# Grouping wide and narrow matmuls by block in the feed-forward products of a two-layer decoder trunk, and building its tables at a later block

## The chip, the cores and the metric

The kernel runs on one core of one Trainium2 chip. The metric is the device time of one execution in microseconds (us). The core has five engines that run their own instruction streams and wait for one another through semaphores: TensorE (PE in the profile; its weight loads are listed as PEld), VectorE (DVE), ScalarE (ACT), GpSimd (POOL) and SyncE (SP), which here only issues DMAs. About 0.2% is what a measurement of this kernel can tell from no change.

## The reference

Two layers work on 256 tokens of width 1024. Each layer is a feed-forward part, a token mixer and a second feed-forward part, each added to the running x. The mixer of layer 0 is a dilated sliding-window attention, that of layer 1 a multi-head latent attention.

```python
D_MODEL, SEQ, DEPTH, D_FF = 1024, 256, 2, 2816

def swiglu(x, w_in, w_out):
    gate, up = jnp.split(x @ w_in, 2, axis=-1)
    return (jax.nn.silu(gate) * up) @ w_out

for i in range(DEPTH):
    x = x + 0.5 * swiglu(rmsnorm(x, norm_gains[i, 0]), ffn_w_in[i, 0], ffn_w_out[i, 0])
    h = rmsnorm(x, norm_gains[i, 1])
    y = dilated_window_attention(h, ...) if i == 0 else latent_attention(h, ...)
    x = x + y
    x = x + 0.5 * swiglu(rmsnorm(x, norm_gains[i, 2]), ffn_w_in[i, 1], ffn_w_out[i, 1])
```

The attention layers also need rotary tables (sines and cosines of the token positions times learned gains).

## The kernel before

**Precision.** Products are taken in a rounded 32-bit format. To keep accuracy, each operand is split into a rounded part `hi` and the rest `lo`: ACT casts a loaded weight piece to `hi` (line 107), DVE subtracts it from the raw piece to get `lo` (line 108). The activations are split in the same way and lie side by side, 256 columns of the rounded part and 256 of the rest. A product then needs two matmuls for each 128x128 weight tile: a **wide** one, in which the `hi` weights meet all 512 columns, and a **narrow** one, in which the `lo` weights meet only the 256 columns of the rounded part. Both add into the same bank of PSUM.

**Stages.** `trunk_kernel` runs a feed-forward part, the dilated attention, two feed-forward parts in a row, the latent attention, and a last feed-forward part. So there are four feed-forward stages, and `ffn` is called four times (lines 1035, 1037, 1039, 1041).

**One feed-forward stage.** The 2816 hidden columns are 22 blocks of 128. For each block `up(c)` takes one weight piece of 1 MB and makes 16 wide and 16 narrow matmuls: 8 slices k of the 1024 inputs, and for each the gate and the up weights (u = 0, 1). `taken` (lines 238, 240) and `gate` (lines 244 to 251) then turn the PSUM sums into the hidden activations `hh`. `down(sweep, q)` takes four hidden blocks and multiplies them into four of the eight output slices: again 16 wide (line 266) and 16 narrow (line 274) matmuls for one weight piece of 1 MB. The first sweep of `down` is interleaved with the `up` blocks, one after every fourth; its last piece and the second sweep follow the last block. I call one `up(c)`, or one full `down`, a **unit**: 16 wide and 16 narrow matmuls.

**Order on PE.** In three of the stages the matmuls of a unit alternate: wide, narrow, wide, narrow. The last stage sets `grouped=True`, and its `up` goes wide, wide, narrow, narrow. `down` alternates in all stages.

**Norm of the input.** The factor of the RMS norm is applied to the product, after the fact, so `up` can start before it is known. Inside early blocks `midway` puts `stats` (line 176: a sum over partitions on PE, then line 178 on DVE and a power on POOL, line 180) and `spread_rstd` (line 187 on DVE, line 189 on PE, line 191 on DVE). In the first stage both are in the third block, at k = 0 and k = 4; in the others they are in the second and third block at k = 4.

**Tables.** `setup` (lines 353 to 418) loads constants, gains and positions, and builds the rotary tables in about fifty small DVE instructions and two ACT ones. It is called by the hook of the first stage ahead of block 4.

**What sets the order.** The Tile framework allocates buffers (4 raw pieces, 3 `hi`, 3 `lo`, 2 PSUM tiles of two banks for `up`) and orders each engine's instructions by its own schedule, except for those that the first stage pins with `keep_in_program_order`. So an instruction can stand earlier or later on its engine than in the program. Each engine then runs its own list strictly in that order.

Of the kernel before, what the change touches and what calls it, by code (L numbers as in the profile page):

```python
# [30 lines left out]
P = 128  # L31
S = 256
D = 1024
KT = D // P
DFF = 2816
NC_FF = DFF // P
# [16 lines left out]
class Trunk:  # L53
# [82 lines left out]
    def squares(self, d0, xs, in_order=False, pinned=False):  # L136

        nc = self.nc
        n = xs.shape[1]
        sq = self.st.tile([P, 2, S], F32, name="sq")  # L140
        if in_order:
            nc.scalar.activation(
                sq[:, :n, :].rearrange("p d (a b) -> p d b a", b=4), xs.rearrange("p d (b a) -> p d b a", b=4), AF.Square
            )
        else:
            self.pin(pinned, nc.scalar.activation(sq[:, :n, :], xs, AF.Square))
        if d0 == 0:
            self.ssq = self.st.tile([P, S], F32, name="ssq")
            nc.gpsimd.tensor_tensor(self.ssq, sq[:, 0, :], sq[:, 1, :], op=ALU.add)
        else:  # L150
            for i in range(n):
                nc.gpsimd.tensor_tensor(self.ssq, self.ssq, sq[:, i, :], op=ALU.add)
# [38 lines left out]
        nc.vector.tensor_copy(self.bc, ps[:, :S])  # L191


    def ffn(self, up_w, out_w, done, first=None, hook=None, grouped=False):
        nc, tc = self.nc, self.tc
        with (
            tc.tile_pool(name="ff", bufs=2) as ff,
            tc.tile_pool(name="hh", bufs=NC_FF) as hp,
            ExitStack() as banks,
        ):  # L200

            acc_banks = self.banks(banks, "acc", 4)
            up_banks = self.banks(banks, "up", 2, other=True)
            self.small = lambda: acc_banks.tile([P, 512], F32, name="acc")
            hs = {}
            xs, xh = self.xs, self.xh

            pieces = {}

            def fetch(c, ahead=None, pinned=False):  # L210
                pieces[c] = self.piece(up_w[c], 4 if c < 6 else 1, ahead, pinned)

            def up(c, midway=()):
                if c not in pieces:
                    fetch(c)
                hi, lo = pieces.pop(c)
                hv, lv = (t.rearrange("p (k u c) -> p k u c", k=KT, u=2) for t in (hi, lo))

                ps = up_banks.tile([P, 2, 2, S], F32, name="up")
                for k in range(KT):  # L220
                    both = xs[:, k].rearrange("p t s -> p (t s)")
                    for part, u in ((0, 0), (0, 1), (1, 0), (1, 1)) if grouped else ((0, 0), (1, 0), (0, 1), (1, 1)):
                        if part == 0:
                            nc.tensor.matmul(  # L224
                                ps[:, u].rearrange("p t s -> p (t s)"), hv[:, k, u, :], both, start=k == 0, stop=False, skip_group_check=True
                            )
                        else:
                            nc.tensor.matmul(  # L228
                                ps[:, u, 0, :], lv[:, k, u, :], xh[:, k, :], start=False, stop=k == KT - 1, skip_group_check=True
                            )  # L230
                    for at, what in midway:
                        if k == at:
                            what()
                return ps

            def taken(ps, pinned=False):
                rest = ff.tile([P, 2, S], F32, name="rest")
                self.pin(pinned, nc.scalar.copy(rest, ps[:, :, 1, :]))  # L238
                gu = ff.tile([P, 2, S], F32, name="gu", bufs=4)
                self.pin(pinned, nc.vector.tensor_tensor(gu, ps[:, :, 0, :], rest, op=ALU.add))  # L240
                return gu

            def gate(c, gu):
                nc.vector.tensor_tensor(gu, gu, self.bc.unsqueeze(1).broadcast_to([P, 2, S]), op=ALU.mult)
                sg = ff.tile([P, S], F32, name="sg")
                nc.scalar.activation(sg, gu[:, 0, :], AF.Silu)
                h = ff.tile([P, S], F32, name="h")
                nc.vector.tensor_tensor(h, sg, gu[:, 1, :], op=ALU.mult)  # L248
                hs[c] = hh = hp.tile([P, 2, S], F32R, name="hh")
                nc.scalar.copy(hh[:, 0, :], h)  # L250
                nc.vector.tensor_tensor(hh[:, 1, :], h, hh.bitcast(F32)[:, 0, :], op=ALU.subtract)  # L251

            def down(sweep, q, accs, finish=None):

                cs = range(4 * q, min(4 * q + 4, NC_FF))
                hi, lo = (
                    t[:, : len(cs) * 512].rearrange("p (c d) -> p c d", d=512)  # L260
                    for t in self.piece(out_w[sweep][:, 4 * q * 512 : (cs[-1] + 1) * 512])
                )

                def term(c, d):
                    ds = slice(d * P, (d + 1) * P)
                    nc.tensor.matmul(  # L266
                        accs[d].rearrange("p t s -> p (t s)"),
                        hi[:, c - cs[0], ds],
                        hs[c].rearrange("p t s -> p (t s)"),
                        start=c == 0,  # L270
                        stop=False,
                        skip_group_check=True,
                    )
                    nc.tensor.matmul(  # L274
                        accs[d][:, 0, :], lo[:, c - cs[0], ds], hs[c][:, 0, :], start=False, stop=c == NC_FF - 1, skip_group_check=True
                    )

                if not finish:
                    for c in cs:
                        for d in range(4):  # L280
                            term(c, d)
                    return
                for ds in finish:
                    for d in ds:
                        for c in cs:
                            term(c, d)
                    done(sweep * 4 + ds[0], len(ds), [accs[d] for d in ds], 0.5)

            gus = {}
            if first:  # L290

                begin, squares = first
                fetch(0, begin, True)
                sums = up(0)
                squares(0)
                squares(1)
                fetch(1, None, True)
                squares(2)
                squares(3)
                gus[0] = taken(sums, True)  # L300
                sums = up(1)
                fetch(2, None, True)
                gus[1] = taken(sums, True)
                sums = up(2, ((0, lambda: self.stats(True)), (4, lambda: self.spread_rstd(True))))
                fetch(3, None, True)
                gus[2] = taken(sums, True)
            else:
                for c, what in enumerate((None, self.stats, self.spread_rstd)):
                    gus[c] = taken(up(c, ((KT // 2, what),) if what else ()))
            for c in range(3):  # L310
                gate(c, gus.pop(c))
            accs = None
            for c in range(3, NC_FF):
                if hook and c == 4:
                    hook()
                gate(c, taken(up(c)))
                if c % 4 == 1:
                    accs = accs or [acc_banks.tile([P, 512], F32, name="acc").rearrange("p (t s) -> p t s", t=2) for _ in range(4)]
                    down(0, c // 4 - 1, accs)
            down(0, 5, accs, ((0, 1), (2, 3)))  # L320
            pairs = [up_banks.tile([P, 2, 2, S], F32, name="up") for _ in range(2)]
            accs = [pairs[d // 2][:, d % 2] for d in range(4)]
            for q in range(5):
                down(1, q, accs)
            down(1, 5, accs, ((0,), (1,), (2,), (3,)))
# [673 lines left out]
def trunk_kernel(ctx: ExitStack, tc: tile.TileContext, x, pos, cst, ident, gtab, up, down, a_qk, a_v, a_out, b_in, b_kv, b_q, b_out, out):  # L999
    nc = tc.nc  # L1000
    t = Trunk(ctx, tc)
# [19 lines left out]
    def then_norm(gcol, order_from=False, order_to=False, columns=S):  # L1021
        def finish(d0, n, acc, scale):
            t.g = gcol
            t.place(columns)
            xs = t.residual(d0, n, acc, scale, order_from)
            t.split_x(d0, xs, order_to)
            t.squares(d0, xs, order_to)

        return finish
# [8 lines left out]
    t.side = "right"  # L1038
    t.ffn(up[2], down[2], then_norm(32, order_to=True))
    t.latent(b_in, b_kv, b_q, b_out, then_norm(40, order_from=True))  # L1040
    t.ffn(up[3], down[3], store, grouped=True)

# [84 lines left out]
```

## Time and profile before

| | us |
|---|---|
| median of 3 runs | 1159.91 (1158.91 to 1160.2) |
| the profiled execution: time | 1159.64 |
| the profiled execution: span, first to last instruction | 1157.9 |
| PE busy | 1141.0 (99% of the span) |
| DVE busy | 847.2 (73%) |
| ACT busy | 644.4 (56%) |

The profile gives, for each instruction, its start and length. Matmuls are pipelined: the start-to-start distance of two of them is what one costs, while the recorded length also holds its way through the array. "idle before" is the time in which the engine stood still ahead of an instruction, and behind the arrow is the instruction whose end let it go on. The granted clock is the share of TensorE's full clock; its mean over the run is 0.997.

### The profile page before, as it was taken

The page shows a single profiled execution, that of the slowest core. Times are in us where ns is not written, and L with a number is a line of the kernel's source. Part 1 is how long each engine was busy: PE and PEld are TensorE (multiplying, and loading weights), DVE is VectorE, ACT ScalarE, POOL GpSimd, SP SyncE. Part 2 cuts the span into 40 slices and gives each one's busy share as a digit, 9 for nine tenths or more (in the row PEclk, how much of TensorE's full clock was granted, in tenths as well). Part 3 has the DMA queues.
Part 4 walks back from the last instruction along what each step waited for, and adds up shares of the span by engine and source line. Part 5 has one row for each costly group of instructions (what it writes and reads, how often), then busy time and mean ns, then how long its engine had stood idle before and what let it go on. Part 6 is the DMA issues. An engine that isn't in the chain of part 4 may idle for free. (4 is left out here: it accounts for less than half of the span.)

```text
span 1157.9 us, 17729 instructions
## 1 busy us (share of the span) xinstructions
PE 1141.0 (99%) x6940; PEld 981.4 (85%) x6940; DVE 847.2 (73%) x1517; ACT 644.4 (56%) x1097; POOL 108.8 (9%) x99
## 2 busy tenths in 40 slices
PE   9899999999999999999999999999999899999998
PEld 8788888787888888888888888888888788888887
DVE  7866666888787977776666686666776897766673
ACT  6554545657566565654554464554555876555541
POOL 2000001221111211200000110000013212000000
PEclk9999999999999999999999999999999999999999
DMA  8555455554444344265555556554443334555550
GB/s 322 215 182 187 166 191 184 186 178 177 151 145 140 121 160 164 80 213 182 185 184 173 190 178 202 193 188 164 164 154 111 110 112 181 182 188 197 177 177 24
DMA packets 29747, 196.20 MB, mean 169 GB/s; under 512 B 3424, under 2 KB 4192, under 8 KB 7136
## 3 DMA queue, kind: packets, MB, share of 16 engines
q1 hardware_dynamic: 29376, 194.55, 48.5%
q8 instruction: 54, 0.88, 0.3%
q10 hardware_dynamic: 288, 0.52, 0.2%
q14 instruction: 29, 0.24, 0.1%
HBM read 194.01 MB, written 1.05 MB: 168 GB/s over the span
## 5 line engine op out<-in xcount | busy, mean ns | idle before, releaser
L108 DVE TENSOR_TENSOR lo<-raw,hi 128x512 fp32r<-128x512 f32 (+3 forms) x412 | 448.6, 1117 | 225.5 <-ACT hi L107 224.5
L107 ACT CAST hi<-raw 128x512 fp32r<-128x512 f32 (+3 forms) x412 | 376.7, 955 | 233.5 <-PE up L224 62.5
L224 PE MATMUL up<-xs,hi 128*128 128x512 f32 x1408 | 489.0, 400 | 1.8 <-DVE xs L134 1.3
L228 PE MATMUL up<-xs,lo 128*128 128x256 f32 x1408 | 367.0, 281 | 2.9 <-DVE lo L108 2.8
L224 PEld LDWEIGHTS up<-xs,hi 128*128 128x128 f32 x1408 | 253.5, 189 | 52.1 <-DVE xs L134 2.4
L228 PEld LDWEIGHTS up<-xs,lo 128*128 128x128 f32 x1408 | 267.2, 190 | 20.5 <-DVE lo L108 4.5
L266 PE MATMUL acc<-hh,hi 128*128 128x512 f32 x352 | 124.9, 395 | 0.0
L266 PE MATMUL up<-hh,hi 128*128 128x512 f32 x352 | 124.3, 394 | 0.3 <-DVE xg L163 0.3
L547 PE MATMUL acc<-hi,xs 128*128 128x512 f32 (+1 forms) x320 | 121.1, 379 | 0.0
L549 PE MATMUL acc<-hi,xs 128*128 128x512 f32 (+1 forms) x320 | 118.5, 370 | 0.0
L548 PE MATMUL acc<-lo,xs 128*128 128x512 f32 (+1 forms) x320 | 118.3, 370 | 0.0
L250 ACT CAST hh<-h 128x256 fp32r<-128x256 f32 x88 | 35.6, 406 | 140.5 <-DVE h L248 140.5
L274 PE MATMUL up<-hh,lo 128*128 128x256 f32 x352 | 99.5, 283 | 0.0
L274 PE MATMUL acc<-hh,lo 128*128 128x256 f32 x352 | 98.9, 282 | 0.0
L266 PEld LDWEIGHTS acc<-hh,hi 128*128 128x128 f32 x352 | 66.0, 188 | 16.0 <-DVE hh L251 1.0
L266 PEld LDWEIGHTS up<-hh,hi 128*128 128x128 f32 x352 | 66.1, 188 | 15.8 <-DVE xg L163 0.9
L547 PEld LDWEIGHTS acc<-hi,xs 128*128 128x128 f32 x320 | 60.3, 188 | 10.9 <-ACT vc L539 0.9
L549 PEld LDWEIGHTS acc<-hi,xs 128*128 128x128 f32 x320 | 60.3, 188 | 9.8
L548 PEld LDWEIGHTS acc<-lo,xs 128*128 128x128 f32 x320 | 60.3, 189 | 9.2
L274 PEld LDWEIGHTS up<-hh,lo 128*128 128x128 f32 x352 | 66.2, 188 | 0.2
L274 PEld LDWEIGHTS acc<-hh,lo 128*128 128x128 f32 x352 | 65.9, 188 | 0.0
L240 DVE TENSOR_TENSOR gu<-up,rest 128x512 f32<-128x512 f32 x88 | 60.1, 683 | 1.5 <-ACT rest L238 1.4
(195 smaller groups left out, 1339.1 us busy)
## 6 DMA issues: line engine op xcount, KB each, us to landing
raw<-in_up SPq DMA_DIRECT2D x87, 1024.0 KB, 4.9
raw<-in_down SPq DMA_DIRECT2D x40, 1024.0 KB, 4.8
raw<-in_a_qk SPq DMA_DIRECT2D x24, 1024.0 KB, 4.9
raw<-in_a_v SPq DMA_DIRECT2D x12, 1024.0 KB, 4.8
raw<-in_down SPq DMA_DIRECT2D x8, 512.0 KB, 3.5
raw<-in_a_out SPq DMA_DIRECT2D x4, 1024.0 KB, 4.8
raw<-in_b_out SPq DMA_DIRECT2D x4, 1024.0 KB, 4.8
raw<-in_b_in SPq DMA_DIRECT2D x3, 1024.0 KB, 5.1
```

The source lines that it names most:

```text
L107: self.pin(pinned, nc.scalar.copy(hi[:, c], raw[:, c]))
L108: self.pin(pinned, nc.vector.tensor_tensor(lo[:, c], raw[:, c], hi.bitcast(F32)[:, c], op=ALU.subtract))
L224: nc.tensor.matmul(ps[:, u].rearrange("p t s -> p (t s)"), hv[:, k, u, :], both, start=k == 0, stop=False, skip_group_check=True)
L228: nc.tensor.matmul(ps[:, u, 0, :], lv[:, k, u, :], xh[:, k, :], start=False, stop=k == KT - 1, skip_group_check=True)
L240: self.pin(pinned, nc.vector.tensor_tensor(gu, ps[:, :, 0, :], rest, op=ALU.add))
L250: nc.scalar.copy(hh[:, 0, :], h)
L266: nc.tensor.matmul(accs[d].rearrange("p t s -> p (t s)"), hi[:, c - cs[0], ds], hs[c].rearrange("p t s -> p (t s)"), start=c == 0, stop=False,
L274: nc.tensor.matmul(accs[d][:, 0, :], lo[:, c - cs[0], ds], hs[c][:, 0, :], start=False, stop=c == NC_FF - 1, skip_group_check=True)
L547: nc.tensor.matmul(out, xh, hi[:, k, :], start=kk == 0, stop=False)
L548: nc.tensor.matmul(out, xh, lo[:, k, :], start=False, stop=False)
L549: nc.tensor.matmul(out, xl, hi[:, k, :], start=False, stop=kk == KT - 1)
```

## The change

Four things are edited.

1. `up` of every block but the first makes all 16 wide matmuls and then all 16 narrow ones. The first block of a stage goes slice by slice in k, each with two wide and then two narrow ones.
2. `down` makes all wide matmuls of a piece first and then all narrow ones; in the last, half-size pieces it does so for each group of output slices that is finished together.
3. The callbacks of `midway` now run behind the narrow matmuls of their slice k, which stand in the second half of a block.
4. The hook of the first stage, which builds the tables, is called ahead of block 12 instead of block 4. The `grouped` flag goes.

```diff
-                for k in range(KT):
-                    both = xs[:, k].rearrange("p t s -> p (t s)")
-                    for part, u in ((0, 0), (0, 1), (1, 0), (1, 1)) if grouped else ((0, 0), (1, 0), (0, 1), (1, 1)):
...
-                    for at, what in midway:
-                        if k == at:
-                            what()
+                def term(k, u, part):
...
+                for ks in [(k,) for k in range(KT)] if c == 0 else [range(KT)]:
+                    for part in range(2):
+                        for k in ks:
+                            for u in range(2):
+                                term(k, u, part)
+                            if part == 1:
+                                for at, what in midway:
+                                    if k == at:
+                                        what()
...
+                def terms(pairs):
+                    for c, d in pairs:
+                        nc.tensor.matmul(
+                            accs[d].rearrange("p t s -> p (t s)"),
+                            hi[:, c - cs[0], d * P : (d + 1) * P],
...
+                    for c, d in pairs:
+                        nc.tensor.matmul(
+                            accs[d][:, 0, :],
+                            lo[:, c - cs[0], d * P : (d + 1) * P],
...
                 if not finish:
-                    for c in cs:
-                        for d in range(4):
-                            term(c, d)
+                    terms([(c, d) for c in cs for d in range(4)])
                     return
                 for ds in finish:
-                    for d in ds:
-                        for c in cs:
-                            term(c, d)
+                    terms([(c, d) for d in ds for c in cs])
                     done(sweep * 4 + ds[0], len(ds), [accs[d] for d in ds], 0.5)
...
-                if hook and c == 4:
+                if hook and c == 12:
                     hook()
...
-    t.ffn(up[3], down[3], store, grouped=True)
+    t.ffn(up[3], down[3], store)
```

The instruction order of the changed kernel has the same instructions as before; what differs is where they stand. The first place is on PE in the first stage, from the second block (bank `up_210`) into the third (bank `up_259`), where `stats` (line 176) stands. Before, with line 224 the wide and 228 the narrow matmul:

```order
L228 MATMUL up_210<-xs_74,lo_188 128x256
L224 MATMUL up_259<-xs_74,hi_244 128x512
L228 MATMUL up_259<-xs_74,lo_245 128x256
L224 MATMUL up_259<-xs_74,hi_244 128x512
L228 MATMUL up_259<-xs_74,lo_245 128x256
L176 MATMUL acc_264<-ones_76,ssq_180 128x1 x2
L224 MATMUL up_259<-xs_74,hi_244 128x512
```

Changed, with line 222 the wide and 231 the narrow matmul; `up_346` is the fourth block:

```order
L222 MATMUL up_210<-xs_74,hi_187 128x512 x16
L231 MATMUL up_210<-xs_74,lo_188 128x256 x16
L222 MATMUL up_259<-xs_74,hi_244 128x512 x16
L231 MATMUL up_259<-xs_74,lo_245 128x256 x2
L176 MATMUL acc_278<-ones_76,ssq_180 128x1 x2
L231 MATMUL up_259<-xs_74,lo_245 128x256 x8
L189 MATMUL acc_296<-dg_293,ones_76 128x256
L231 MATMUL up_259<-xs_74,lo_245 128x256 x6
L222 MATMUL up_346<-xs_74,hi_307 128x512 x16
```

A unit is now one run of 16 wide and one run of 16 narrow matmuls. Between `stats` and `spread_rstd` (line 189) there stood 16 matmuls of both kinds before (8 wide, 8 narrow); now there are 8 narrow ones.

The second place is on DVE in the first stage. Before, the table instructions (lines 377 to 416) stand between the parts of `lo_458`, the `lo` weights of the fifth block:

```order
L108 TENSOR_TENSOR lo_458<-raw_456,hi_457 128x512
L248 TENSOR_TENSOR h_386<-sg_384,gu_381 128x256
L380 TENSOR_SCALAR sq_399<-sq_399 128x192
L395 SCALAR_TENSOR_TENSOR tB_417<-sq_400,gt_393 128x32 x2
L381 TENSOR_TENSOR sq_399<-sq_399 128x192
L251 TENSOR_TENSOR hh_388<-h_386,hh_388 128x256
L382 TENSOR_SCALAR sq_399<-sq_399 128x192
L395 SCALAR_TENSOR_TENSOR tB_417<-sq_400,gt_393 128x32 x5
L392 SCALAR_TENSOR_TENSOR tA_416<-sq_400,gt_393 128x32 x8
```

Seventeen more table instructions follow, the last of them ahead of the rest of the weights (`lo_515` is the sixth block's):

```order
L413 SCALAR_TENSOR_TENSOR tAq_434<-sq_400,gt_393 128x16
L416 SCALAR_TENSOR_TENSOR tBq_435<-sq_400,gt_393 128x16
L413 SCALAR_TENSOR_TENSOR tAk_436<-sq_400,gt_393 128x16
L416 SCALAR_TENSOR_TENSOR tBk_437<-sq_400,gt_393 128x16
L108 TENSOR_TENSOR lo_458<-raw_456,hi_457 128x512
L108 TENSOR_TENSOR lo_515<-raw_513,hi_514 128x512 x4
```

Changed, the first of them stand here; `lo_651` and `lo_702` are the `lo` weights of the ninth and tenth block, and `up_553` is the bank of the seventh:

```order
L108 TENSOR_TENSOR lo_651<-raw_649,hi_650 128x2048
L262 TENSOR_TENSOR hh_502<-h_500,hh_502 128x256
L382 CAST pf_897<-pi_895 128x4
L419 SCALAR_TENSOR_TENSOR tAq_934<-gt_893 128x64
L386 TENSOR_SCALAR sq_899<-cst_891,pf_897 128x48 x4
L419 SCALAR_TENSOR_TENSOR tAq_934<-gt_893 128x64
L387 TENSOR_SCALAR sq_899<-sq_899 128x192
L388 TENSOR_SCALAR sq_899<-sq_899 128x192
L390 SCALAR_TENSOR_TENSOR sq_899<-sq_899 128x192 x2
L108 TENSOR_TENSOR lo_702<-raw_700,hi_701 128x2048
L251 TENSOR_TENSOR gu_588<-up_553,rest_586 128x512
L390 SCALAR_TENSOR_TENSOR sq_899<-sq_899 128x192
```

The table instructions have moved behind the fifth and sixth block's weights, and are spread over several of the later pieces. On SP the three loads of the tables' inputs move from ahead of the fifth block's weight load to behind that of the first `down` piece. Beyond the first stage the lists of DVE, ACT and POOL differ by a few neighbours that change places, and SP's not at all.

More of the change, by code (lines that the diff above doesn't have):

```diff
@@ L191, in spread_rstd, with ffn @@
         nc.vector.tensor_copy(self.bc, ps[:, :S])
-    def ffn(self, up_w, out_w, done, first=None, hook=None, grouped=False):
+    def ffn(self, up_w, out_w, done, first=None, hook=None):
         nc, tc = self.nc, self.tc
@@ L219, in up @@
                 ps = up_banks.tile([P, 2, 2, S], F32, name="up")
-                for k in range(KT):
-                    both = xs[:, k].rearrange("p t s -> p (t s)")
-                    for part, u in ((0, 0), (0, 1), (1, 0), (1, 1)) if grouped else ((0, 0), (1, 0), (0, 1), (1, 1)):
[L223 to L230, printed above, removed]
-                    for at, what in midway:
-                        if k == at:
-                            what()
+                def term(k, u, part):
+                    if part == 0:
+                        nc.tensor.matmul(
+                            ps[:, u].rearrange("p t s -> p (t s)"),
+                            hv[:, k, u, :],
+                            xs[:, k].rearrange("p t s -> p (t s)"),
+                            start=k == 0,
+                            stop=False,
+                            skip_group_check=True,
+                        )
+                    else:
+                        nc.tensor.matmul(
+                            ps[:, u, 0, :], lv[:, k, u, :], xh[:, k, :], start=False, stop=k == KT - 1, skip_group_check=True
+                        )
+                for ks in [(k,) for k in range(KT)] if c == 0 else [range(KT)]:
[7 more added lines that the diff above has]
+                                        what()
                 return ps
@@ L262, in down @@
                 )
[L264 to L276, printed above, removed]
+                def terms(pairs):
+                    for c, d in pairs:
+                        nc.tensor.matmul(
+                            accs[d].rearrange("p t s -> p (t s)"),
+                            hi[:, c - cs[0], d * P : (d + 1) * P],
+                            hs[c].rearrange("p t s -> p (t s)"),
+                            start=c == 0,
+                            stop=False,
+                            skip_group_check=True,
+                        )
+                    for c, d in pairs:
+                        nc.tensor.matmul(
+                            accs[d][:, 0, :],
+                            lo[:, c - cs[0], d * P : (d + 1) * P],
+                            hs[c][:, 0, :],
+                            start=False,
+                            stop=c == NC_FF - 1,
+                            skip_group_check=True,
+                        )
                 if not finish:
-                    for c in cs:
-                        for d in range(4):
-                            term(c, d)
+                    terms([(c, d) for c in cs for d in range(4)])
                     return
                 for ds in finish:
-                    for d in ds:
-                        for c in cs:
-                            term(c, d)
+                    terms([(c, d) for d in ds for c in cs])
                     done(sweep * 4 + ds[0], len(ds), [accs[d] for d in ds], 0.5)
```

## The prediction

> **What bounds the kernel now.** I read the page first, then the order of time on PE, then the one long wait of PE.
>
> ```profile
> span 1157.9 us, 17729 instructions
> ...
> PE 1141.0 (99%) x6940; PEld 981.4 (85%) x6940; DVE 847.2 (73%) x1517; ACT 644.4 (56%) x1097; POOL 108.8 (9%) x99
> ...
> L107 ACT CAST hi<-raw 128x512 fp32r<-128x512 f32 (+3 forms) x412 | 376.7, 955 | 233.5 <-PE up L224 62.5
> ```
>
> PE never rests, and ACT, which prepares the weights, waits for PE to give buffers back. So the time is what PE's list costs, matmul by matmul, plus the few places where it waits. Start-to-start distances tell the first. In the order of time on PE a row is: start, length, line, matmul, count. Three places in the first stage:
>
> ```profile
> 76.21 0.39 PE L266 MATMUL acc<-hh,hi 128*128 128x512 f32 x1
> ...
> 81.83 0.40 PE L224 MATMUL up<-xs,hi 128*128 128x512 f32 x1
> ...
> 87.48 0.40 PE L224 MATMUL up<-xs,hi 128*128 128x512 f32 x1
> ...
> 93.13 0.40 PE L224 MATMUL up<-xs,hi 128*128 128x512 f32 x1
> 93.37 0.28 PE L228 MATMUL up<-xs,lo 128*128 128x256 f32 x1
> ...
> 94.19 0.40 PE L224 MATMUL up<-xs,hi 128*128 128x512 f32 x1
> ```
>
> A `down` unit lasts 81.83 - 76.21 = 5.62 us and an `up` unit 87.48 - 81.83 = 5.65; three alternating pairs last 1.06, or 353 ns a pair. The last stage, which goes in twos, is faster with the same matmuls:
>
> ```profile
> 1019.02 0.62 PE L224 MATMUL up<-xs,hi 128*128 128x512 f32 x2
> 1019.49 0.40 PE L228 MATMUL up<-xs,lo 128*128 128x256 f32 x2
> ...
> 1024.60 0.63 PE L224 MATMUL up<-xs,hi 128*128 128x512 f32 x2
> ```
>
> Its unit lasts 5.58 us. Longer stretches of three `up` units and a `down` unit, from the windows (stretch, length, busy time of each engine), give finer figures:
>
> ```profile
> 59.25:81.83 22.58, 22.58 (x131) 19.64 (x129) 15.67 (x19) 11.70 (x14) 0.00 (x0) 1.00 0.57 189
> ...
> 1013.45:1035.79 22.34, 22.34 (x131) 19.51 (x130) 15.61 (x18) 11.67 (x14) 0.00 (x0) 1.00 0.54 190
> ```
>
> An `up` unit is (22.58 - 5.62) / 3 = 5.653 in the first stage and (22.34 - 5.62) / 3 = 5.573 in the last, 353 against 348 ns a pair. So the order alone is worth 5 ns a pair here.
>
> **Term 1: the pace of a unit.** No unit of 16 and 16 is in the trace; long runs of one width are, in the attention stages:
>
> ```profile
> 221.29 0.40 PE L549 MATMUL acc<-hi,xs 128*128 128x512 f32 x1
> ...
> 236.26 0.39 PE L549 MATMUL acc<-hi,xs 128*128 128x512 f32 x1
> ...
> 871.34 0.39 PE L945 MATMUL acc<-hi,ch 128*128 128x512 f32 x1
> ...
> 874.12 0.50 PE L798 MATMUL ob<-ones,kt 128*128 128x1 f32 x4
> 876.07 0.28 PE L118 MATMUL acc<-xs,hi 128*128 128x256 f32 x1
> ...
> 880.62 0.28 PE L120 MATMUL acc<-xs,lo 128*128 128x256 f32 x1
> ```
>
> The first two rows are 66 wide matmuls apart: 14.97 / 66 = 227 ns. The last two are 38 narrow ones apart: 4.55 / 38 = 120. Between them stand 12 wide ones behind a narrow run: 2.78 / 12 = 232. A unit of 16 and 16 so costs 16 x (227 + 120) = 5.55 at best and 16 x (232 + 120) = 5.63 at worst. The last stage's 5.573 lies near the lower end, with eight changes of width where the new unit has one. I take **5.56** and keep 5.52 to 5.63 (the lower end lets narrow ones keep the 115 to 119 that some show).
>
> The count: 59 `up` units of the first three stages run steadily at 5.653 (22 each, less the first block of each stage, the second and third of the first stage, and the second and third of the third, which wait for x or run faster already), 21 in the last at 5.573, and 4 x 11 = 44 `down` units at 5.62 (4 x 176 pairs; small last pieces counted in). Before, that is 333.5 + 117.0 + 247.3 = 697.8 us; at 5.56, 124 x 5.56 = 689.4. **Gain 8.4 us**; at 5.52, 13.3; at 5.63, -0.3.
>
> **Term 2: the wait for the tables.** The list of PE's waits between 30 and 46 us has one row; below it are PE's and DVE's rows around it, and the windows with the granted clock (the number after the engines):
>
> ```profile
> PE up L228 <- DVE lo L108: 2.8, 1, 2.8
> ```
>
> ```profile
> 25.87 0.39 PE L224 MATMUL up<-xs,hi 128*128 128x512 f32 x1
> ...
> 40.69 0.42 PE L228 MATMUL up<-xs,lo 128*128 128x256 f32 x1 [2.75 <-DVE lo L108]
> ...
> 53.62 0.39 PE L224 MATMUL up<-xs,hi 128*128 128x512 f32 x1
> ```
>
> ```profile
> 36.98 0.25 DVE L382 TENSOR_SCALAR sq<-sq 128x192 f32<-128x192 f32 x1
> ...
> 39.96 0.68 DVE L108 TENSOR_TENSOR lo<-raw,hi 128x512 fp32r<-128x512 f32 x1
> ```
>
> ```profile
> 41.00:44.00 3.00, 3.00 (x11) 2.61 (x11) 3.00 (x5) 1.14 (x1) 0.00 (x0) 0.50 0.78 243
> ...
> 675.00:678.00 3.00, 2.22 (x13) 1.71 (x12) 3.00 (x6) 0.95 (x2) 0.83 (x1) 1.00 0.97 309
> ```
>
> DVE spends 36.98 to 39.96 on tables, the fifth block's last `lo` part comes behind them, and PE stands 2.75 us. Then PE runs at a clock of 0.50 for some 3 us. From the fourth block (25.87) to the seventh (53.62) three blocks and a `down` unit take 27.75 us, where 3 x 5.65 + 5.62 = 22.57 would do: the stall costs 5.2, of which 2.75 is the wait and the rest mostly the slow clock.
>
> With the tables moved, what is late next? By the order DVE has the tenth block's `lo` as next work when it takes the seventh block's result, so it is two units and more ahead. The steady stretch of four units above leaves it 22.58 - 15.67 = 6.9 us free, and no more than some 17 table instructions stand ahead of one `lo`, about 1.7 us at the 2.98 / 30 = 0.1 us that one takes in the stretch above. Narrow matmuls now come second, so `lo` may be 16 x 0.23 = 3.6 us later besides. I cost the tables at 0; if this cover fails, up to the 5.2 comes back. The two ACT table steps and the three loads on SP go the same way: SP's list then runs ahead of need, its next piece waits for a buffer anyway. **Gain 5.2 us.**
>
> The clock bears on a new wait below. The Trainium skill's TensorE: Matmul & The Clock Gate, Part 1, says that the clock halves after about 3.4 us of idleness. The trace agrees roughly: a wait of 2.75 us halved it, while the 3.00 - 2.22 = 0.78 us of waiting in the window 675 to 678 left it at 1.00. Were every wait to halve it, the new wait below would cost some 1.7 us more; I count none.
>
> **Term 3: start of the first stage.**
>
> ```profile
> 6.13 0.79 PE L224 MATMUL up<-xs,hi 128*128 128x512 f32 x1 [0.50 <-ACT hi L107]
> 6.85 0.58 PE L228 MATMUL up<-xs,lo 128*128 128x256 f32 x1
> 7.23 0.63 PE L224 MATMUL up<-xs,hi 128*128 128x512 f32 x1
> ...
> 13.85 0.39 PE L224 MATMUL up<-xs,hi 128*128 128x512 f32 x1
> ...
> 19.40 0.39 PE L224 MATMUL up<-xs,hi 128*128 128x512 f32 x1
> ```
>
> The first narrow matmul waits 0.72 for `lo`, where the next rows are 0.43 apart; in the new order the second wide one fills that: -0.3. The new wait is in the third block, between `stats` and `spread_rstd`:
>
> ```profile
> 21.36 0.14 DVE L178 TENSOR_SCALAR var<-acc 128x2 f32<-128x2 f32 x1
> ```
>
> ```profile
> 21.58 0.71 POOL L180 TENSOR_TENSOR rstd<-var,mhalf 128x2 f32<-128x2 f32 x1 [1.90 <-DVE var L178]
> ```
>
> ```profile
> 22.32 0.48 DVE L187 TENSOR_SCALAR dg<-ident,rstd 128x128 f32<-128x128 f32 x2 [0.82 <-POOL rstd L180]
> ```
>
> From 21.36 to 22.80 this chain takes 1.44 us, and with the hand-over about 1.6; 8 narrow matmuls cover 8 x 0.12 = 0.96. PE waits **0.7**, at least 0.4 and at most 1.6 with no cover. Six narrow matmuls and the fourth block queue behind; DVE's `bc` and the fourth block's `lo` too, but those are needed 3.6 us into that block. Net of the start: 0.3 - 0.7 = -0.4. In the other stages a whole unit stands between the two, as before.
>
> **Sum.** 8.4 + 5.2 - 0.4 = 13.2 us. From the profiled execution's 1159.64 (its span of 1157.9 and 1.7 around it) that leaves 1146.4. The median of the three runs is 0.3 above that execution, so I forecast **1146.7**. Stage starts that wait for x, and the attention stages, I leave as they are.
>
> **Rivals.**
> - *The order of widths is worth nothing.* For it: the second block of the first stage, alternating, took 19.40 - 13.85 = 5.55, so alternation can run at the best pace, and 12 wide ones behind a narrow run took 232 each. Against it: the steady units of the last stage are 0.08 shorter than the others. It leaves 5.2 - 0.4 from the median: 1155.1. [...] Chance 0.14.
> - *The stall moves.* The tables hold up a later block's `lo`, with wait and slow clock: the 5.2 comes back, 1151.9. The lead of two units speaks against it. Chance 0.06.
> - *Narrow runs go faster*, 5.52 a unit: 1141.8. Chance 0.09.
> - *Slower: wide runs never settle.* Each change to a wide run could hold it at the slowest alternating gap seen, 0.24 (93.13 to 93.37): 16 x (0.24 + 0.12) = 5.76 a unit, 124 x 5.76 = 714.2, a loss of 16.4; less 4.8, 1171.5. It decides from 5.67 a unit, where 124 units cost 4.8 more than before. The 227 of 66 wide ones in a row speak against it. Chance 0.03.
> - *It does not do what it says*: the order shows runs of 16, so I give it nothing of its own.
>
> **How the numbers follow.** The forecast, a unit at 5.54 to 5.60 and no stall (1144.2 to 1151.7), has 0.68. The range 1141.5 to 1154.0 takes in the fast narrow runs and the moved stall and leaves out 0.17. What a measurement can tell from no change is about 0.2%, 2.3 us: faster needs less than 1157.6. All cases but the slow one and a little of the first rival's upper side lie there: faster 0.95, same 0.02, slower 0.03.
>
> **What would show it.** In the changed profile: units of 5.56 between first wide matmuls of neighbouring blocks (wide 227 to 230 apart, narrow 120); no PE wait for DVE `lo` around 40 us and the clock at 1.00 there; the seventh block starting near 48.5 instead of 53.62; a wait of PE for DVE `dg` of about 0.7 near 25. The prediction fails if units stay at 5.62 or more, or if a wait for `lo` shows between 50 and 120 us.

## The result and the profile after

The changed kernel takes 1150.99 us (median of 4 runs, 1150.21 to 1151.43), against 1159.97 for the kernel before in the same session: a ratio of 0.9924, 95% interval 0.9906 to 0.9941. That is a gain of 9.0 us where 13.2 were forecast; the time lies inside the range, and on the side that had 0.95.

The page of the changed kernel, from its profiled execution (1150.89 us):

```profile
span 1149.1 us, 17728 instructions
...
PE 1132.7 (99%) x6940; PEld 981.0 (85%) x6940; DVE 846.6 (74%) x1517; ACT 645.9 (56%) x1097; POOL 111.8 (10%) x99
...
L107 ACT CAST hi<-raw 128x512 fp32r<-128x512 f32 (+3 forms) x412 | 375.3, 955 | 224.3 <-PE up L222 100.3
```

PE is still busy for 99% of the span, with the same 6940 matmuls, and ACT still waits for PE. So the gain must again be read from the order of time on PE. In the first stage (start, length, line, matmul, count; 222 and 231 are the wide and narrow matmul of `up`, 277 and 286 those of `down`):

```profile
31.90 3.82 PE L222 MATMUL up<-xs,hi 128*128 128x512 f32 x16
...
37.47 3.82 PE L222 MATMUL up<-xs,hi 128*128 128x512 f32 x16
41.12 2.08 PE L231 MATMUL up<-xs,lo 128*128 128x256 f32 x16
43.03 3.88 PE L277 MATMUL acc<-hh,hi 128*128 128x512 f32 x16
46.75 2.09 PE L286 MATMUL acc<-hh,lo 128*128 128x256 f32 x16
48.67 0.63 PE L222 MATMUL up<-xs,hi 128*128 128x512 f32 x2
```

An `up` unit lasts 37.47 - 31.90 = 5.57 us, as forecast: 3.65 / 16 = 228 ns for a wide matmul, 1.91 / 16 = 119 for a narrow one. But the `down` unit lasts 48.67 - 43.03 = 5.64, a little more than the 5.62 of before: its wide matmuls take 3.72 / 16 = 232. The seventh block starts at 48.67 instead of 53.62 (forecast: 48.5).

The list of PE's waits between 30 and 130 us is empty. Between 15 and 30 it has one row. Below it are the windows around the old stall (length, busy time of each engine, granted clock, DMA share, GB/s) and PE's rows around the new wait:

```profile
PE acc L189 <- DVE dg L187: 0.5, 1, 0.5
```

```profile
36.00:39.00 3.00, 3.00 (x21) 2.74 (x20) 3.00 (x7) 2.81 (x4) 0.00 (x0) 1.00 0.59 169
39.00:42.00 3.00, 3.00 (x19) 2.61 (x18) 3.00 (x4) 0.97 (x2) 0.00 (x0) 1.00 0.91 295
```

```profile
23.40 1.19 PE L231 MATMUL up<-xs,lo 128*128 128x256 f32 x8
25.10 0.70 PE L189 MATMUL acc<-dg,ones 128*128 128x256 f32 x2 [0.50 <-DVE dg L187]
...
26.34 0.86 PE L222 MATMUL up<-xs,hi 128*128 128x512 f32 x3
```

No stall near 40 us, and the clock there at 1.00. The new wait for `dg` is there: 0.50 by the row, and counted from start to start 25.10 - 23.40 - 8 x 0.12 = 0.74, since the idle time counts only from the modelled end of the last matmul. The granted clock stayed at 1.00 through it.

Where the 8.8 us between the two spans went, by the starts of the same matmuls in the two traces, summed over the four stages (gains are rounded from finer figures):

| stretch | before | after | gain | forecast |
|---|---|---|---|---|
| blocks 4 to 22 with the five full `down` units between them, without the stall | 517.9 | 513.3 | 4.6 | 8.4 with the next row |
| last pieces of the first sweep, and the second sweep | 162.4 | 163.1 | -0.8 | |
| stall of the tables | 5.2 | 0 | 5.2 | 5.2 |
| first three blocks | 76.7 | 77.2 | -0.6 | -0.4 |
| the attention stages, by difference | | | 0.4 | 0 |

All of the shortfall stands in the first term, the pace of a unit; and the rows above say in which units: `down`.

### The profile page after: what moved, and what is told of

It reads as the page before. It is cut to its first block, busy times and chain, and to the rows that moved or that the text cites. A ratio compares the mean times of both kernels' runs of the same rounds, so it can differ in the third digit from the quotient of the medians.

```text
span 1149.1 us, 17728 instructions
## 1 busy us (share of the span) xinstructions
PE 1132.7 (99%) x6940; PEld 981.0 (85%) x6940; DVE 846.6 (74%) x1517; ACT 645.9 (56%) x1097; POOL 111.8 (10%) x99
## 5 line engine op out<-in xcount | busy, mean ns | idle before, releaser
L222 PE MATMUL up<-xs,hi 128*128 128x512 f32 x1408 | 341.6, 391 | 3.6 <-DVE xs L134 2.7
L222 PEld LDWEIGHTS up<-xs,hi 128*128 128x128 f32 x1408 | 256.5, 188 | 52.8 <-DVE xs L134 2.8
L231 PEld LDWEIGHTS up<-xs,lo 128*128 128x128 f32 x1408 | 184.8, 191 | 10.4 <-DVE lo L108 1.2
L231 PE MATMUL up<-xs,lo 128*128 128x256 f32 x1408 | 189.7, 283 | 0.0
L277 PE MATMUL up<-hh,hi 128*128 128x512 f32 x352 | 88.7, 396 | 0.3 <-DVE xg L163 0.3
L277 PE MATMUL acc<-hh,hi 128*128 128x512 f32 x352 | 87.4, 396 | 0.0
L149 POOL TENSOR_TENSOR ssq<-sq 128x256 f32<-128x256 f32 x6 | 10.7, 1784 | 515.1 <-ACT sq L146 365.9
L255 DVE TENSOR_TENSOR gu<-gu,bc 128x512 f32<-128x512 f32 x88 | 60.0, 686 | 1.0
L717 POOL TENSOR_TENSOR rr<-r,mhalf 128x8 f32<-128x8 f32 x24 | 39.2, 1637 | 194.2 <-DVE r L715 194.2
L249 ACT COPY rest<-up 128x512 f32<-128x512 f32 x88 | 50.7, 577 | 5.4 <-PE up L231 4.1
```

The costliest lines, as they stand in the source:

```text
L222: nc.tensor.matmul(ps[:, u].rearrange("p t s -> p (t s)"), hv[:, k, u, :], xs[:, k].rearrange("p t s -> p (t s)"), start=k == 0, stop=Fals ...
L231: nc.tensor.matmul(ps[:, u, 0, :], lv[:, k, u, :], xh[:, k, :], start=False, stop=k == KT - 1, skip_group_check=True)
L277: nc.tensor.matmul(accs[d].rearrange("p t s -> p (t s)"), hi[:, c - cs[0], d * P : (d + 1) * P], hs[c].rearrange("p t s -> p (t s)"), star ...
```

## The experiments

Each ran beside the kernel before, whose median was 1159.7 to 1160.4. "Unit" is the median distance of the first wide matmuls of neighbouring full units in the trace, which tells 0.01 us apart where the time doesn't tell 1 us; for `down` the first sweep's 20 units and the second sweep's.

| run | us | ratio to before, 95% | `up` | `down`, sweep 1 / 2 |
|---|---|---|---|---|
| before | 1159.97 | | 5.650 | 5.614 / 5.618 |
| changed | 1150.99 | 0.9906 to 0.9941 | 5.567 | 5.641 / 5.619 |
| e1_down_alternating | 1149.35 | 0.9899 to 0.9930 | 5.567 | 5.608 / 5.620 |
| e2_down_one_bank | 1151.46 | 0.9920 to 0.9952 | 5.567 | 5.641 / 5.619 |
| e3_down_two_banks | 1151.16 | 0.9914 to 0.9945 | 5.566 | 5.641 / 5.619 |
| e4_down_diagonal | 1151.30 | 0.9920 to 0.9956 | 5.567 | 5.641 / 5.619 |
| e5_down_reads_x | 1149.83 | 0.9895 to 0.9928 | 5.567 | 5.567 / 5.619 |
| e6_wides_joined | 1149.95 | 0.9898 to 0.9928 | 5.566 | see there |
| e7_hook_at_5th | 1151.07 | 0.9908 to 0.9938 | 5.567 | 5.641 / 5.619 |
| e8_hook_alone | 1154.80 | 0.9941 to 0.9971 | 5.650 | 5.614 / 5.620 |
| e9_hidden_512 | 1148.54 | 0.9878 to 0.9921 | 5.567 | 5.567 / 5.567 |
| e10_hidden_256 | 1149.10 | 0.9884 to 0.9920 | 5.567 | 5.567 / 5.567 |
| e11_all | 1147.84 | 0.9877 to 0.9910 | 5.567 | 5.567 / 5.567 |
| e12_alternating_512 | 1155.91 | 0.9946 to 0.9974 | 5.650 | 5.650 / 5.654 |

### Is it the order inside down?

The first guess was the order of output banks: `up` alternates between two, `down` goes through four. Four kernels changed nothing but the order of `down`:

```diff
-                    terms([(c, d) for c in cs for d in range(4)])
+                    for c in cs:                                     # e1 (the last pieces likewise)
+                        for d in range(4):
+                            terms([(c, d)])
+                    terms([(c, d) for d in range(4) for c in cs])    # e2
+                    terms([(c, d) for d2 in (0, 2) for c in cs for d in (d2, d2 + 1)])            # e3
+                    terms([(cs[(d + i) % 4 if q else i], d) for i in range(4) for d in range(4)])  # e4
```

> The down products go back to pairs of a wide and a narrow matmul; up products, tables and all else as in the changed kernel. Theory A (wide matmuls of down that go through four output banks in turn stay at 232 ns, so that grouping costs down 0.02 to 0.03 us a unit): its units come back from 5.64 and 5.62 to 5.615, some 44 x 0.02 = 1 us, so about 1150 us. Rival (grouping is neutral for down, and something else of the changed kernel slows it): units stay at 5.62 to 5.64 and the time at 1151. The up units stay at 5.567 by both.

> Down units still 16 wide, then 16 narrow, but four matmuls in a row go to one output bank, and the moving operand changes with each. Theory A (the turn through four banks holds the wide ones at 232 ns): wide 227, a unit 5.56 to 5.57, 40 units x 0.07 = 2.8 us less: about 1148.2. Theory B (what settles a run is that the moving operand is used again by the next matmul): wide 232 or more, 5.64 or more, 1151 or above. Theory C (the place of the hidden values or the work beside down): unchanged, 5.62 to 5.64, 1151.

> Down units still 16 wide, then 16 narrow, in the pattern of an up unit: two output banks in turn, the moving operand used by two matmuls in a row (banks 0 and 1 for the four blocks, then banks 2 and 3). Theory A: wide 227, a unit 5.57, about 1148.2. Theory B (moving operand used again): 5.57 as well, as in the up units. Theory C (place of the hidden values or the work beside down): unchanged, 5.62 to 5.64, 1151.

> Down units still 16 wide, then 16 narrow, through four output banks in turn, but with another moving operand for each matmul (the second to fifth piece of each sweep; the first piece and the last, short one as in the changed kernel). Theory A (four banks in turn): wide stay at 232, 5.62 to 5.64, 1151. Theory B (the same moving operand four times in a row is what slows down): wide 227, 5.57, 32 units x 0.07 = 2.2 us less, 1148.8. Theory C (place of the hidden values or the work beside down): unchanged, 1151.

e1 brought the first sweep back to 5.61, so grouping did cost `down` its 0.03 us a unit, 20 x 0.033 = 0.7 us. (Its time fell by 1.6; the rest is at the start of the third stage, which waits for x: its first three blocks took 19.0 us instead of 20.5.) e2, e3 and e4 fell flat, and with them theory A (by e2 and e3) and theory B (by e3 and e4). Four orders of banks and operands gave the same distances to about a nanosecond. Below are the 16 distances of a unit's wide matmuls in ns, medians over the 20 `down` units of the first sweep, and for comparison over the `up` units of the changed kernel:

```
changed  231 233 241 232 231 232 228 230 233 241 233 231 232 228 230 232
e2       231 233 241 232 231 232 228 230 233 241 233 231 232 228 230 232
e3       231 232 241 232 231 232 228 230 232 241 232 231 232 228 230 232
e4       231 232 241 232 231 232 228 230 232 241 233 231 232 228 230 232
up       233 236 228 233 231 227 227 227 227 227 227 227 227 227 227 227
```

A pattern that doesn't care which bank is written and which hidden block is read belongs to something that all of `down`'s matmuls have in common, and `up`'s don't.

### Is it what down reads?

Two theories were left: a run keeps the rhythm that its first gaps give it (D), or something in the operands of `down` holds it at 232 (C). e5 lets the first sweep read pieces of x instead of the hidden values; e6 puts the wide matmuls of `down` straight behind settled wide ones of `up`.

```diff
-                            hs[c].rearrange("p t s -> p (t s)"),
+                            (xs[:, c % KT] if other else hs[c]).rearrange("p t s -> p (t s)"),   # e5, sweep 0
...
+                        if part == 1 and between:        # e6, in up: between = (0, c // 4 - 1, accs)
+                            terms = down(*between)
+                            terms[0]()                   # the wide ones of down; terms[1], the narrow ones, behind up's
```

> In the first sweep the full down units (20 of them) read pieces of x as moving operand instead of the hidden values, so the output differs; the second sweep is as in the changed kernel and serves as control. Theory C (reading the hidden values, their place or their fresh writing, keeps the wide matmuls at 232): first-sweep units fall from 5.641 to 5.56 to 5.57, the second sweep's stay at 5.62; 20 x 0.075 = 1.5 us less, 1149.5. Theory D (a run keeps the rhythm that its first gaps give it, whatever it reads): first-sweep wide matmuls stay at 232 and the unit at 5.64, 1151.

> In the first sweep 16 wide matmuls of an up unit are followed by the 16 wide ones of the down unit behind it, then the 16 narrow ones of up and the 16 of down. Theory D (a run keeps the rhythm that its first gaps give it): the down wides carry on at 227 behind settled up wides, 20 units x 0.08 = 1.6 us less, 1149.4. Theory C (something that down reads or writes keeps it at 232): they return to 231 to 233 with 241 in between, 1151.

PE in order of time, first e5, then e6 (line 284 is there the wide matmul of `down`, 295 the narrow one):

```profile
37.62 3.82 PE L222 MATMUL up<-xs,hi 128*128 128x512 f32 x16
...
43.19 3.82 PE L277 MATMUL acc<-xs,hi 128*128 128x512 f32 x16
46.84 2.08 PE L286 MATMUL acc<-xs,lo 128*128 128x256 f32 x16
48.76 1.55 PE L222 MATMUL up<-xs,hi 128*128 128x512 f32 x6
```

```profile
37.16 3.82 PE L222 MATMUL up<-xs,hi 128*128 128x512 f32 x16
40.81 3.89 PE L284 MATMUL acc<-hh,hi 128*128 128x512 f32 x16
44.53 2.06 PE L231 MATMUL up<-xs,lo 128*128 128x256 f32 x16
...
48.33 1.99 PE L222 MATMUL up<-xs,hi 128*128 128x512 f32 x8
```

Reading x, the `down` unit lasts 48.76 - 43.19 = 5.57, the same as an `up` unit; the second sweep of the same kernel, which reads the hidden values, stayed at 5.62. And behind settled wide matmuls the hidden values slow PE at once: 40.81 to 44.53 is 3.72 / 16 = 232. The sequence is another one there (distances that alternate between about 238 and 229 ns), but its mean is the same, so what goes with the operands is the pace and not the sequence. Theory D is out, although e6's time of 1149.95 lies nearer to its 1149.4 than to theory C's 1151: the joined pair of units lasts 48.33 - 37.16 = 11.17 us where the two last 5.567 + 5.641 = 11.21 apart, 20 x 0.04 = 0.8 in all, at an unchanged pace of the wide `down` matmuls. It is the hidden values as moving operand.

### Their content, their age, or their place?

What sets them apart can be read from the built program: where its tiles begin in a partition of SBUF.

```
tile     first byte   past a multiple of 512
xs            35328     0    (pieces of 2048 bytes)
hi, lo        88576, 113152     0
hh           163712   384    (22 tiles of 2048 bytes, all 384 past)
ch, cl       207744, 212864   384    (latent attention, stationary operand)
```

An unused tile ahead of them in the same pool moves the hidden values, and nothing else that PE reads:

```diff
+            ff.tile([P, 32], F32, name="pad", bufs=1)     # e9: 128 bytes; e10: [P, 96], 384 bytes
             hs = {}
```

> The changed kernel with an unused tile of 128 bytes ahead of the hidden values, so that each of them begins at a multiple of 512 bytes in its partition (before, 384 past one), as the pieces of x do. Theory E (a moving operand that begins off a multiple keeps the wide matmuls at 232): down units fall to 5.567 in both sweeps, 20 x 0.074 + 20 x 0.052 + the short last pieces, some 2.7 us less: about 1148.3. Rival F (their place high in the partition, beside the tiles that VectorE and ScalarE write, or their fresh writing): unchanged, 5.64 and 5.62, 1151.

> The same with 384 bytes, so that the hidden values begin 256 past a multiple of 512. Theory E in its wide form (a multiple of 256 is enough): 5.567 and about 1148.3; in its narrow form (512 is needed): another rhythm, 5.60 to 5.65, 1150 to 1151. Rival F: unchanged, 5.64 and 5.62, 1151.

PE in e9 (line 278 is the wide matmul of `down`, 287 the narrow one):

```profile
42.81 3.82 PE L278 MATMUL acc<-hh,hi 128*128 128x512 f32 x16
46.47 2.08 PE L287 MATMUL acc<-hh,lo 128*128 128x256 f32 x16
48.38 2.00 PE L223 MATMUL up<-xs,hi 128*128 128x512 f32 x8
```

48.38 - 42.81 = 5.57, and both sweeps run at 5.567. The time fell by 1150.99 - 1148.54 = 2.45 us; 20 x 0.074 + 20 x 0.052 = 2.5, and some 2.7 with the last pieces, were expected. e10 did the same to the units with an offset of 256, so a multiple of 256 is enough. Rival F (place high in the partition, fresh writing) is out: the tiles moved by 128 bytes and are written as before.

The Trainium skill, SBUF — State Buffer, section Operand start alignment, asks only that an operand start at a multiple of its element size, and says that its runs timed nothing. 384 is such a multiple, and here it costs 5 ns of each wide matmul in a grouped run (232 against 227).

### What is the order worth, then?

> The kernel before (alternating matmuls) with the tables at the thirteenth block and the 128 bytes ahead of the hidden values. It asks what the order is worth to down units when every operand begins at a multiple of 512. If alternating pairs cost what they cost in the up units, whose operands begin so already (353 ns a pair), down units stay at 5.61 to 5.65 and the time at 1155 to 1156.5 (1154.8 is the time without the 128 bytes). Rival: the offset was what slowed the alternating down units too, and they settle at 5.55 to 5.57: 40 x 0.055 = 2.2 us less, 1152.6, so that the order of widths is worth nothing to down.

```diff
-                if hook and c == 4:
+                if hook and c == 12:
+            ff.tile([P, 32], F32, name="pad", bufs=1)
```

First and last matmul of a `down` unit in this kernel, and the next block (lines 267, 275 and 225):

```profile
43.09 0.40 PE L267 MATMUL acc<-hh,hi 128*128 128x512 f32 x1
...
48.63 0.28 PE L275 MATMUL acc<-hh,lo 128*128 128x256 f32 x1
48.74 0.40 PE L225 MATMUL up<-xs,hi 128*128 128x512 f32 x1
```

48.74 - 43.09 = 5.65: with aligned operands `down` alternates as slowly as `up` does, and 1.1 us more than without the 128 bytes (1154.80). So the two things act together; a `down` unit in the first sweep lasts

| | alternating | grouped |
|---|---|---|
| hidden values 384 past a multiple of 512 | 5.614 | 5.641 |
| at a multiple of 512 | 5.650 | 5.567 |

Grouping gains 0.083 us a unit over the steady pace of alternation where operands begin at a multiple, and loses 0.027 in the first sweep where they begin 384 past one. The change met the first case in `up` and the second in `down`. In the second sweep it changes nothing at 384 (5.618 and 5.619); why the two sweeps differ is open.

Two alternating blocks don't fit the table. They are the second and the fourth block of the first stage in the kernel before, which read x at a multiple of 512 like all of `up`. The end of the fourth:

```profile
31.07 0.40 PE L224 MATMUL up<-xs,hi 128*128 128x512 f32 x1
31.30 0.28 PE L228 MATMUL up<-xs,lo 128*128 128x256 f32 x1
31.42 0.39 PE L224 MATMUL up<-xs,hi 128*128 128x512 f32 x1
```

They lasted 19.40 - 13.85 = 5.55 and 31.42 - 25.87 = 5.55 us, the pace of a grouped unit. In e8 and e12 the fourth block lasted 5.65, as the steady `up` blocks of the alternating stages do. So alternation can run fast. What tips it into the slower pace is not known.

### Do the two halves of the change add up?

> The changed kernel with the tables back at the fifth block of the first stage. If the tables' place is worth what the first term of the stall says, the wait for lo and the slow clock come back with 4.9 us: about 1156. Rival: narrow matmuls now stand last in a unit, so lo is needed later, by 0.9 us for its last quarter (3.64 + 12 x 0.12 = 5.1 instead of 12 x 0.353 = 4.2 us into the unit): a wait of 1.9 us, and if the clock stays at 1.00 behind that, about 1153.

> The kernel before with only the tables moved to the thirteenth block. If the parts of the change add up: 4.9 us less than before, about 1155, no wait for lo near 40 us, the seventh block at 48.7. Rival (in the alternating order lo is needed earlier, so the tables hold up a later block): part of the stall shows behind the thirteenth block, 1156 to 1159.

```diff
-                if hook and c == 12:
+                if hook and c == 4:      # e7: the changed kernel with the old place
...
-                if hook and c == 4:
+                if hook and c == 12:     # e8: the kernel before with the new place
```

e8 came out as forecast: 1154.80, 5.2 less than before. e7 did not: 1151.07, the time of the changed kernel, with no wait of PE for `lo` and the clock at 1.00. Neither theory had that. PE's rows in e7, and DVE's first `lo` part behind the tables:

```profile
35.95 3.82 PE L222 MATMUL up<-xs,hi 128*128 128x512 f32 x16
39.60 0.62 PE L277 MATMUL acc<-hh,hi 128*128 128x512 f32 x2
40.12 1.34 PE L231 MATMUL up<-xs,lo 128*128 128x256 f32 x8
41.30 0.39 PE L277 MATMUL acc<-hh,hi 128*128 128x512 f32 x1
```

```profile
39.40 0.67 DVE L108 TENSOR_TENSOR lo<-raw,hi 128x512 fp32r<-128x512 f32 x1
```

```profile
39.00:42.00 3.00, 3.00 (x19) 2.46 (x18) 3.00 (x11) 0.65 (x1) 0.00 (x0) 1.00 0.00 0
```

DVE is done with the tables at 39.40, about as late as before (39.96). But PE has work that needs no `lo`: 16 wide matmuls of the block up to 39.60, and then wide ones of `down`, which the schedule has put ahead of and between the narrow ones in PE's list, so that these stand where their `lo` parts arrive (DVE delivers the first from 39.40 to 40.07, and the first narrow matmul stands at 40.12). Blocks four to six and the `down` unit take 22.62 us, 0.3 more than in the changed kernel. So grouping alone removes the stall and nearly all of its 5.2 us; moving the tables as well adds nothing that the time shows. Each half of the change is enough for the stall.

### Together

```diff
+            ff.tile([P, 32], F32, name="pad", bufs=1)        # hidden values
+            la.tile([P, 32], F32, name="pad", bufs=1)        # ch, cl
-                            if part == 1:
-                                for at, what in midway:
-                                    if k == at:
-                                        what()
+                            for at, what, *early in midway:
+                                if k == at and part == (0 if early else 1):
+                                    what()
-                sums = up(2, ((0, lambda: self.stats(True)), (4, lambda: self.spread_rstd(True))))
+                sums = up(2, ((4, lambda: self.stats(True), True), (4, lambda: self.spread_rstd(True))))
```

> The changed kernel with the 128 bytes ahead of the hidden values, the same in the latent attention (its ch and cl tiles, there the stationary operand, then begin at multiples of 512 as well), and stats of the first stage issued among the wide matmuls of the third block, so that 24 matmuls instead of 8 stand between it and spread_rstd. Theory E: down units 5.567; the wait for dg near 24 us, 0.5 us of the page, is gone; the 12-matmul runs of the latent attention settle at 227 if the rule holds for the stationary operand too: together 2.7 + 0.8 + 0.4, about 1147.1. Rival F: only the wait goes, 1150.3.

A run of 12 wide matmuls in the latent attention: its first row, its seventh, and the row behind its last; the changed kernel, then e11:

```profile
862.47 0.39 PE L958 MATMUL acc<-hi,ch 128*128 128x512 f32 x1
...
863.87 0.40 PE L958 MATMUL acc<-hi,ch 128*128 128x512 f32 x1
...
865.25 0.50 PE L811 MATMUL ob<-ones,kt 128*128 128x1 f32 x4
```

```profile
860.71 0.40 PE L959 MATMUL acc<-hi,ch 128*128 128x512 f32 x1
...
862.10 0.39 PE L959 MATMUL acc<-hi,ch 128*128 128x512 f32 x1
...
863.46 0.50 PE L812 MATMUL ob<-ones,kt 128*128 128x1 f32 x4
```

Over the last six 1.38 / 6 = 230 against 1.36 / 6 = 227: the run now settles, and its first distances too are those of an `up` unit (234, 236, 228 instead of 231, 232, 228). All twelve take 2.75 us instead of 2.78. The moving operands, `hi` and `lo`, are where they were, so the place of the stationary operand counts as well. The wait for `dg` is gone; the third block in e11, then in e9:

```profile
19.88 2.46 PE L223 MATMUL up<-xs,hi 128*128 128x512 f32 x10
22.17 0.50 PE L176 MATMUL acc<-ones,ssq 128*128 128x1 f32 x4
...
25.18 0.59 PE L189 MATMUL acc<-dg,ones 128*128 128x256 f32 x2
...
26.32 2.00 PE L223 MATMUL up<-xs,hi 128*128 128x512 f32 x8
```

```profile
18.91 3.82 PE L223 MATMUL up<-xs,hi 128*128 128x512 f32 x16
...
24.86 0.70 PE L189 MATMUL acc<-dg,ones 128*128 128x256 f32 x2 [0.50 <-DVE dg L187]
...
26.11 1.09 PE L223 MATMUL up<-xs,hi 128*128 128x512 f32 x4
```

With 1147.84 us this is the fastest kernel of the study, 3.2 below the changed one, though 0.7 above the 1147.1 expected. Against e9 it is 0.7 better, which one comparison hardly tells apart. The third block says more: 26.32 - 19.88 = 6.44 us against 26.11 - 18.91 = 7.20, so the earlier `stats` bought the 0.8 that was expected. The first two blocks, which this edit doesn't touch, took 0.5 longer in e11's trace than in e9's, and hide most of it in the sum of the three (19.84 and 20.06).

## Why the prediction was right, and where it fell short

**Term 1, the pace of a unit: right in kind, too large by 4.6 us.** Its mechanism held for `up`, 5.567 against 5.56, with wide runs that settle at 227 and narrow ones at 120; that was worth some 5.1 of the 5.8 us counted for it. The step that failed is the one that let every wide run settle alike: the "44 `down` units at 5.62" were taken to 5.56 like the others, for 2.6 us. They went to 5.64 and 5.62 instead (the prediction's own sign of failure, "units stay at 5.62 or more", so came true for `down` and not for `up`), and with the short last pieces and the second sweep they cost 0.5 + 0.8 = 1.3 us. Of the 3.9 us between, 2.5 are the 128 bytes by which the hidden values stand off a multiple of 256: e9 gives them back. The rest lies around the last pieces, which were not taken apart further.

The sign of it stood in the prediction's own rows. 66 wide matmuls at 227 and 12 at 232 were read as the two ends of one range, the second put down to the narrow run ahead. They were two cases: the 66 read x, at a multiple of 256, and the 12 read `ch`, 384 past a multiple of 512. e11 shows that the 12, behind the same narrow run, settle at 227 once `ch` is moved.

**Term 2, the stall of the tables: right in size (5.2 forecast, 5.2 found, 5.2 by e8), but not in what removes it.** The prediction gave the gain to the tables' new place alone and added it to term 1. e7 shows that the new order alone removes it too. The sum took no harm, because the two share one gain and it was counted once; that was luck, not reasoning.

**Term 3, the first three blocks of the first stage: -0.5 (19.75 to 20.23) against -0.4**, with the wait for `dg` at 0.74 against 0.7, and a granted clock of 1.00 through it. The prediction counted nothing for the clock, and here that was right. But a rule by the length of a wait can't be read from these traces. Behind the 2.75 us in the kernel before the clock was 0.50, and behind the 0.50 for `dg` it stayed at 1.00. Between them lies one wait of 1.98 us in the latent attention, which all fourteen traces have, and it went both ways. In eleven of them, the changed kernel's among them, some 3.4 us at 0.50 begin near its end; in e5, e7 and e9 none do. The wait and a window behind it, in the changed kernel and then in e9:

```profile
895.18 0.81 PE L871 MATMUL wk<-ident,qn 128*96 128x128 f32 x4 [1.98 <-ACT qt L874]
...
895.60:898.60 3.00, 3.00 (x12) 2.25 (x10) 2.21 (x13) 1.51 (x4) 1.01 (x1) 0.50 0.52 216
```

```profile
893.17 0.64 PE L872 MATMUL wk<-ident,qn 128*96 128x128 f32 x4 [1.98 <-ACT qt L875]
...
893.60:896.60 3.00, 2.87 (x15) 1.84 (x14) 2.21 (x13) 2.05 (x6) 1.01 (x1) 1.00 0.51 210
```

**The rivals.** That the order is worth nothing is refuted by `up` and, more sharply, by e12 against e9: 1155.91 against 1148.54 with the same place of operands and the tables at the same block, 7.4 us for the order alone. What spoke for it, an alternating block at 5.55, stays unexplained. The Trainium skill's TensorE: Matmul & The Clock Gate, section Back-to-back issue gap, gives the gap of an isolated warm matmul by its width alone. In the runs here a wide and a narrow matmul together take 348 ns grouped and 353 alternating (5.567 and 5.650 us by 16), and another time again where the moving operand begins elsewhere. The stall did not move to a later block. Narrow runs stayed at 120. The slow rival, wide runs that never settle, was real in `down`, but at 232 instead of 240, and so 5.64 and not 5.76 a unit, below the 5.67 from which it would have decided.

## What to carry to other kernels

When one loop of a kernel settles at a better pace than another with the same instruction shapes, compare where their operands begin before blaming the order: the first bytes of the tiles are in the built program, and a padding tile tests it in one run. An order of instructions and a placement of buffers can have a joint effect of either sign, so an edit measured under one of them says little of the other. And where two parts of a change could each remove the same stall, count that gain once, and run each part alone before telling which of them did it.

## What the runs showed of the hardware

- A wide matmul (128x128 weights, 512 columns, rounded 32-bit) in a long run settles at 227 ns when both operands begin at a multiple of 256 bytes in their partition, and takes 232 in the mean when the moving one begins 384 past a multiple of 512 (e9, e10 against the changed kernel). The stationary one at 384 does much the same (230 to 232, e11). Offsets other than 0, 256 and 384 were not tried, and why 128 bytes matter stays open.
- The slow case is regular. In the first sweep a sequence of distances repeats every seven matmuls (231, 232, 228, 230, 233, 241, 233), the same in four orders of work and nearly so in the latent attention. In the second sweep and behind a settled run (e6) the sequence is another one, with the same mean of 232, and in e6 it sets in at once.
- In steady pairs of a wide and a narrow matmul the offset works the other way in the first sweep: 5.614 us a unit off the multiple, 5.650 on it (e8 and e12). Two alternating blocks of the kernel before ran at 5.55 on it; the cause is open.
- The same wait of 1.98 us of TensorE was followed by a granted clock of 0.50 in eleven traces and by 1.00 in three.
